# Layer A's product of probabilities and v of pairs 0 to 4, placed before the end of the next pair's key projection

## The chip, the cores and the metric

The kernel runs on one core of a Trainium2 chip. A core has TensorE (PE, with its weight loads as a row of their own, PEld), VectorE (DVE), ScalarE (ACT), GpSimd (POOL) and SyncE (SP), whose queue issues nearly all DMAs here. The metric is the device time of one execution in microseconds, as the median of several runs. A profile is one further execution, recorded by the hardware profiler.

## The reference

The reference is a block of two layers on a sequence of 512 tokens, 1024 wide, in float32. Each layer is RMS norm, an input projection, a mixer over 16 heads of 64, a gate, an output projection and a residual. Layer A, in which the change lies, is attention over dilated windows, for three groups of heads (`g`) that are merged by their softmax denominators:

```python
proj = hn @ w_in                                   # q, k, v of three groups, and the gate
q = rms_norm(q, q_gain[g]); k = rms_norm(k, k_gain[g])
logits = q @ k.T * scale + bias                    # keys within the window of group g
p = exp(logits - max); denom = sum(p)
out = (p @ v) / denom
...
y = sum(alpha[g] * out[g]) * silu(gate)            # alpha: softmax over the groups' log denominators
x = x + y @ w_out
```

Layer B is a neighbourhood attention on an 8 x 64 grid of the same tokens. The change does not touch it.

## The kernel before

**Numbers.** A matrix product of the projections is made of three TensorE matmuls: each operand is split into a high part in fp32r and the rest, and high x high, high x rest and rest x high are summed in PSUM (`mm3`, L232). Three such matmuls of 128 x 128 by 128 x 512 are one step below. The weights come by DMA in raw pieces (`wraw`, L191), ScalarE or VectorE casts them (`wh`, L127), and VectorE or POOL subtracts (`wl`, L133). There are four buffers for `wh` and four for `wl`.

**Layer A's main work.** The sixteen heads are done as eight pairs (`hc` 0 to 7). For a pair, `main_a` (L628) runs in this order: the key projection (`project_qk` with "rawk", 8 values of k times 4 token tiles, 32 steps, which also makes v of groups 1 and 2), the query projection ("rawq", 32 steps), the projection of v of group 0 (`v0_a`, L589, 8 steps) and that of the gate (`gate_a`, L578, 8 steps). In a projection of keys or queries the four token tiles accumulate in the four banks of the pool `ps_acc`; at the last k, after each step, ScalarE evacuates its tile (`evac`, L504, with the activations of L530), and POOL squares it for the norm of the heads. `v0_a` and `gate_a` take a bank of the same pool each (L299).

**Layer A's side work.** Beside this runs the attention of the pair before. The queries and keys of a pair go through DRAM to be turned (`move_q`, L684: a write at L691, four reads at L697); then `split_q` (L736) scales them on ScalarE. `attn_a` (L886) makes the scores in two halves `u` of two token tiles each, both heads side by side, in the four banks of the pool `ps_side` (`bank`, L78), with the softmax on VectorE (L929, L940, L801) and ScalarE (L951, L802). The probabilities are turned by VectorE (L865) and by a write and four reads through DRAM for each half (`turner.send`, L874 and L878). What remains of a pair is put off in the list `pending`: the product of the turned probabilities with v (`weigh`, L962, 52 matmuls into two banks of `ps_side`), then `whole` (L778: a ScalarE copy and a VectorE add that empty the two banks) and `put_y` (L804: the product with the gate on VectorE, y's high part by ScalarE at L827, the rest by POOL at L828).

**What sets the order.** TensorE's order is the order of the text. The others are ordered by the library's scheduler with a simulated timeline (`schedule_with_timeline_sim=True`), but for instructions that `keep_in_program_order` pins behind the one before them on their engine. Main and side work are two Python generators. Main yields after each step; `run` (L1032) then lets the side go on if its due time has come. Time is `clock`, which the helper `matmul` (L222) advances by a modelled duration: 640 for a step, 2,880 for the product of a pair, 1,600 for half of its scores. A side generator gives a number (wait so long), nothing (1,200) or

```python
yield "wait", ("rawk", hc + 1), 5200
```

that is: until 5,200 after the clock at which ("rawk", hc + 1) was stamped, at the end of the key projection of pair `hc + 1`. `later_on` puts DMAs and a few other jobs at a clock as well. `moved(hc)` is true for pairs 0 to 5.

In `attn_a(hc)` of pairs 1 to 5 the first thing done was the product of the pair before, so its place was the beginning of the query projection of pair `hc + 1`, ahead of the first half of the scores of pair `hc`. The product of pair 5 stands in another branch, that of pair 6 too.

Of the kernel before, what the change touches and what calls it, by code (L numbers as in the profile page):

```python
# [51 lines left out]
def tile_hybrid_encoder(  # L52
# [193 lines left out]
    def later_on(delay, job):  # L246

        timers.append((clock[0] + delay, job))
        timers.sort(key=lambda t: t[0])
# [172 lines left out]
    def square_a(k):  # L422
        nc.scalar.activation(x_all[:, k, :], x_all[:, k, :], AF.Square)
# [462 lines left out]
    def attn_a(hc):  # L886
# [7 lines left out]
        def scores(u):  # L894

            tiles = []
            for t in (2 * u, 2 * u + 1):
                cs, n = (64, 192) if t == 0 else (0, 192) if t == 3 else (0, 256)
                tiles.append((t, [bank("log") for _ in range(2)], cs, n))
            for t, lgs, cs, n in tiles:  # L900
                ks = slice(P * t + cs, P * t + cs + n)
                parts = [(0, j, slice(cs, cs + n), k0[:, ks]) for j in range(4)] + [
                    (1 + g, j, slice(256 + P * g, 384 + P * g), qt[:, :, 4 + g, 32 * j : 32 * j + 32])
                    for g in range(2)
                    for j in range(4)
                ]
                for g, j, cols, keys in parts:
                    for hd in range(2):
                        hs = slice(64 * hd, 64 * hd + 64)
                        matmul(  # L910
                            lgs[hd][32 * j : 32 * j + 32, cols],
                            qt[hs, t, g, 32 * j : 32 * j + 32],
                            keys[hs],
                            share=2,
                            start=(g == 0),
                            stop=(g == 2),
                        )
            return [
                (hd, t, softmax(hd, t, lgs[hd], cs, n)) for t, lgs, cs, n in tiles for hd in range(2)
            ]  # L920
# [34 lines left out]
        def turn_p(hd, t, pr):  # L955
            tp = bank("tp")
            for i in range(4):
                transpose(tp[:, i * P : (i + 1) * P], pr[:, i * P : (i + 1) * P])
            dst = sb(pts[0], at(t, 0, hd, 0), [[128, 2], [32, 2], [512, 4], [1, 32]])
            nc.vector.tensor_copy(dst, tp.rearrange("p (g i a r) -> p g i a r", g=2, i=2, a=4))  # L960
# [31 lines left out]
        if hc < NHC - 1:  # L992
            for u in range(2):
                if moved(hc):
                    if pending and u == 0:
                        pending.pop(0)()
                        yield
                    yield "wait", ("rawk", hc + 1), 5200 if u == 0 else 16800 if hc else 12500
                else:
                    yield 6500 if u == 0 else 7000  # L1000
                turned = turner(512)
                turners.append(turned)
                for hd, t, pr in scores(u):
                    turned.put(pr, 512, 256 * hd + 64 * (t % 2), 128)
                send = partial(turned.send, pq[:, 2048 * u : 2048 * u + 2048], *((6000, 500) if u else (8500, 1200)))
                later_on(7000 + 2000 * u, send)
                if pending and u == 0:
                    yield 5000
                    pending.pop(0)()
            pending.append(lambda: put_y(hc, weigh(), True, False))  # L1010
        else:
            for u in range(2):
                if u == 0:
                    yield "wait", ("gate", hc), 500
                yield 600
                held = scores(u)
                yield 3200
                if pending:
                    yield "wait", ("gate", hc - 1), 16800
                    pending.pop(0)()  # L1020
                    yield
                for args in held:
                    turn_p(*args)
                    yield
            yield from v_a(hc)
            stamp["ya", "turned"] = 0
            put_y(hc, weigh(), True, True)
            yield

    pending = []  # L1030
# [258 lines left out]
    def side():  # L1289
        for k in range(KT):  # L1290
            norm(0, k, x_all[:, k, :])
            if k:
                square_a(k - 1)
            stamp["na", k] = 0
            if k == 4:
                gains()
            yield 1000
        square_a(KT - 1)
        for k in range(1, KT):
            yield 1300  # L1300
            nc.vector.tensor_add(x_all[:, 0, :], x_all[:, 0, :], x_all[:, k, :])
        yield 1500
        row_scale(row_sums(x_all[:, 0, :]))
        y = big.tile([P, 2 * KT * S], F32R, tag="y", name="y").rearrange("p (n k t) -> p n k t", n=2, k=KT)
        st["y_h"], st["y_l"] = y[:, 0], y[:, 1]
        yield 2500
        bias_lines()
        later_on(21000, lambda: st.__setitem__(("e", 0), bias_a(0)))
        yield 2500
        scales_a()  # L1310
        first_out()
        stamp["rs", "a"] = 0
        for hc in range(NHC):
            if hc < NHC - 1:
                yield from k_a(hc)
                yield from chain(q_a(hc), v_a(hc))
                if moved(hc):
                    yield from st.pop(("land", hc))
                yield from attn_a(hc)
                if hc == 1:  # L1320
                    bias_rows()
            else:
                gap[0] = cycle((500, 500, 700))
                yield from chain(q_a(hc), k_a(hc))
                yield from attn_a(hc)
        yield from residual(xg, 0)
        yield from residual(xg, 4)
        stamp["ya", KT - 1, "y"] = 0
        yield "wait", ("x", KT - 1), 800
        for f in range(KT):  # L1330
            square_b(f)
            yield 600
        yield 4500
        row_scale(row_sums(st.pop("ssq")))
        stamp["rs", "b"] = 0
        yield 5000
        nc.scalar.mul(rs_half, spread(), 0.5)
        stamp["rs", "all"] = 0
        for job, hc, delay in B_PLAN:
            yield "wait", ("b", "start"), delay  # L1340
            if job == "scores":
                yield from side_b(hc)
                continue
            yield "wait", ("back", hc), 3500
            if hc == NHC - 2:
                stamp["yb", "turned"] = 0
            pending.pop(0)()
            yield
            if hc >= NHC - 2:
                yield from residual(xm_d, 4 * (hc % 2))  # L1350

    run(main(), side())


# [98 lines left out]
```

## Time and profile before

| | before |
|---|---|
| median of 3 runs | 815.26 us (815.03 to 816.6) |
| the profiled execution | 817.6 us |
| its span, from the first instruction to the last | 815.8 us |
| TensorE busy (matmuls) | 808.5 us, 99% |
| VectorE busy | 532.0 us, 65% |
| ScalarE busy | 434.6 us, 53% |
| POOL busy | 246.9 us, 30% |
| DMA | 169.33 MB, mean 208 GB/s |
| layer A's pairs 1 to 4, from one product to the next | about 62 us each |

A line of the profile names the source line, the engine, the operation, the tiles written and read (`acc<-wh,hn_h`), shapes and counts. `acc` are the projections, `log` the scores, `o` the product, `tp` transposes on TensorE, `p` the probabilities. The busy time of TensorE counts each matmul from its start to a modelled end, and matmuls overlap; a busy share of 99% therefore does not say that TensorE never waits. The chain of waits shows better where it does: it goes from the last instruction back to whatever each step waited for. In brackets stands how long an engine was idle before an instruction, and what ended that.

### The profile page before, as it was taken

Reading aid. Unit: us, or ns where it says so; the run is one execution under the profiler, and the core shown is the slowest. Engines: PE = TensorE matmul, PEld = TensorE weight load, DVE = VectorE, ACT = ScalarE, POOL = GpSimd, SP = SyncE. Lnnn points to the kernel's source line nnn. Section 1 sums busy time; section 2 is a strip of 40 time slices with the busy share of each in tenths; the row PEclk is TensorE's granted clock in tenths of the full one; section 3 lists DMA queues with packets and bytes.
Section 4 is the critical chain, followed back from the end, with each engine's and each line's share of the span. In section 5 each row is a group of like instructions: output and inputs, shape, how many; then the busy total and the mean of one; then the engine's idle time right before and its main releaser. Section 6 shows DMA issues by size and latency. Waiting matters only on the chain.

```text
span 815.8 us, 16172 instructions
## 1 busy us (share of the span) xinstructions
PE 808.5 (99%) x5972; PEld 662.2 (81%) x5972; DVE 532.0 (65%) x1364; ACT 434.6 (53%) x913; POOL 246.9 (30%) x400
## 2 busy tenths in 40 slices
PE   9999999999999999999999999999999999999998
PEld 7888888788888888888788888888888887778787
DVE  7466575665576576477476765538656989897824
ACT  7352752752752752662662564536337665757821
POOL 2262441542441441441432342111221315040100
PEclk9999999999999999999999999999999999999999
DMA  7367879779879779968858555157353887698664
GB/s 261 106 207 232 224 216 266 208 200 301 210 210 316 195 220 292 240 186 277 226 164 233 179 160 135 41 193 250 119 164 129 245 230 213 200 268 244 174 213 155
DMA packets 86478, 169.33 MB, mean 208 GB/s; under 512 B 7504, under 2 KB 45520, under 8 KB 86400
## 3 DMA queue, kind: packets, MB, share of 16 engines
q1 hardware_dynamic: 86256, 168.04, 70.0%
q8 instruction: 47, 0.77, 0.4%
q10 hardware_dynamic: 144, 0.26, 0.1%
q14 instruction: 31, 0.25, 0.1%
HBM read 126.21 MB, written 48.22 MB: 214 GB/s over the span
## 4 chain that ended last, share of the span: by engine, by line
PE 92%; DVE 3%; ACT 3%; DMA 1%; issue 1%; SPq 0%; DVEq 0%
PE acc L226 82%; PE log L226 5%; PE o L226 4%; ACT p L1222 1%; PE tp L230 1%; ACT p L1228 1%; DVE wl L133 1%; DMA eb<-eb_d 1%; DMA x_all<-in_xt 0%; DVE rawq L330 0%; DVE rawq L716 0%; PE pa L226 0%; DVE tr L865 0%; ACT wh L127 0%; PE pk L226 0%
## 5 line engine op out<-in xcount | busy, mean ns | idle before, releaser
L226 PE MATMUL acc<-wh,hn_h 128*128 128x512 f32 x704 | 278.8, 397 | 1.2 <-ACT hn_h L419 0.8
L226 PE MATMUL acc<-wl,hn_h 128*128 128x512 f32 x704 | 274.4, 391 | 0.0
L226 PE MATMUL acc<-wh,hn_l 128*128 128x512 f32 x704 | 274.3, 390 | 0.0
L127 ACT CAST wh<-wraw 128x512 fp32r<-128x512 f32 (+1 forms) x240 | 146.2, 613 | 227.0 <-PE acc L226 204.1
L133 DVE TENSOR_TENSOR wl<-wraw,wh 128x512 fp32r<-128x512 f32 (+1 forms) x169 | 121.7, 721 | 132.8 <-ACT wh L127 131.7
L133 POOL TENSOR_TENSOR wl<-wraw,wh 128x512 fp32r<-128x512 f32 (+1 forms) x72 | 94.3, 1310 | 237.8 <-ACT wh L127 228.4
L226 PEld LDWEIGHTS acc<-wh,hn_h 128*128 128x128 f32 x704 | 132.6, 189 | 32.9 <-issue 3.3
L226 PEld LDWEIGHTS acc<-wh,hn_l 128*128 128x128 f32 x704 | 132.7, 189 | 28.0
L226 PEld LDWEIGHTS acc<-wl,hn_h 128*128 128x128 f32 x704 | 132.8, 189 | 26.3
L308 POOL TENSOR_TENSOR sq<-rawq 128x256 f32<-128x256 f32 (+1 forms) x80 | 63.4, 806 | 87.1 <-ACT rawq L530 76.3
L226 PE MATMUL acc<-y,wh 128*128 128x512 f32 (+1 forms) x272 | 81.5, 383 | 0.0
L226 PE MATMUL acc<-hn_h,wh 128*128 128x512 f32 x192 | 75.5, 393 | 0.0
L226 PE MATMUL acc<-hn_l,wh 128*128 128x512 f32 x192 | 74.7, 389 | 0.0
L226 PE MATMUL acc<-hn_h,wl 128*128 128x512 f32 x192 | 74.7, 389 | 0.0
L865 DVE STREAM_TRANSPOSE tr<-p 128x512 f32<-128x512 f32 (+1 forms) x88 | 58.2, 677 | 19.8 <-ACT p L1228 9.0
L311 DVE TENSOR_REDUCE ss<-sq 128x4 f32<-128x256 f32 (+1 forms) x96 | 48.3, 505 | 34.3 <-POOL sq L308 27.4
L951 ACT ACTIVATE p<-p,mn 128x512 f32<-128x512 f32 (+1 forms) x64 | 44.9, 702 | 25.5 <-DVE mn L940 25.5
L226 PEld LDWEIGHTS acc<-y,wh 128*128 128x128 f32 x272 | 48.8, 188 | 9.4 <-issue 0.9
L330 DVE TENSOR_TENSOR rawq<-rawq,rs 128x256 f32<-128x256 f32 (+1 forms) x96 | 51.2, 593 | 5.3 <-POOL rs L119 4.9
L226 PE MATMUL acc<-y,wl 128*128 128x512 f32 (+1 forms) x136 | 51.3, 377 | 0.0
L530 ACT ACTIVATE rawq<-acc,rs_n 128x512 f32<-128x512 f32 (+1 forms) x76 | 44.2, 611 | 0.7 <-PE acc L226 0.2
L802 ACT ACTIVATE p<-p,mn 128x512 f32<-128x512 f32 (+1 forms) x64 | 43.4, 699 | 0.8 <-DVE mn L801 0.7
(142 smaller groups left out, 950.2 us busy)
## 6 DMA issues: line engine op xcount, KB each, us to landing
wraw<-in_w SPq DMA_DIRECT2D x111, 512.0 KB, 5.3
td<-tr SPq DMA_DIRECT2D x14, 1024.0 KB, 6.2
pt<-td SPq DMA_DIRECT2D x56, 256.0 KB, 6.4
qd<-rawq SPq DMA_DIRECT2D x6, 1536.0 KB, 6.6
qt<-qd SPq DMA_DIRECT2D x24, 384.0 KB, 7.4
td<-tr SPq DMA_DIRECT2D x8, 896.0 KB, 4.8
pt<-td SPq DMA_DIRECT2D x32, 224.0 KB, 6.5
v0x<-in_w SPq DMA_DIRECT2D x8, 512.0 KB, 6.0
```

The lines of the kernel that those rows point to most:

```text
L127: nc.scalar.copy(h, raw)
L133: eng.tensor_sub(l, raw, h.bitcast(F32))
L226: nc.tensor.matmul(o, l, r, **kw)
L230: nc.tensor.transpose(o, i, ident)
L308: nc.gpsimd.tensor_mul(sq.rearrange("p (f a r) -> p a f r", a=4, r=32), v, v)
L311: nc.vector.tensor_reduce(ss[:, i * ns : (i + 1) * ns], sq.rearrange("p (a b) -> p a b", b=64), axis=AX.X, op=ALU.add)
L330: m = nc.vector.tensor_mul(v, v, by)
L530: nc.scalar.activation(dst, src, AF.Copy, scale=rs_n[:, i : i + 1])
L802: nc.scalar.activation(pr, pr, AF.Copy, scale=mn[:, 3:4])
L865: nc.vector.transpose(dst, src[:, :n].rearrange(order, b=4, k=32, **({"g": 2} if apart else {})))
L951: nc.scalar.activation(row, row, AF.Exp, bias=mn[:, 1:2], scale=-1.0, accum_out=mn[:, 2:3])
L1222: nc.scalar.activation(pr[:, o : o + n], pr[:, o : o + n], AF.Exp, bias=mn[:, 0:1], scale=-1.0, accum_out=mn[:, 2:3])
```

## The change

Two edits. The product leaves its place at the start of `attn_a`; in its stead `side` gives it a wait of its own, 18,500 after the stamp of the gate of pair `hc`, between the turning of that pair's queries (`q_a`) and the point where they are split (`land`). `pending` is empty for pair 0; for pairs 1 to 5 it holds the product of the pair before.

```diff
@@ attn_a, for u in range(2)
                 if moved(hc):
-                    if pending and u == 0:
-                        pending.pop(0)()
-                        yield
                     yield "wait", ("rawk", hc + 1), 5200 if u == 0 else 16800 if hc else 12500
                 else:
                     yield 6500 if u == 0 else 7000
@@ side, for hc in range(NHC)
                 yield from k_a(hc)
                 yield from chain(q_a(hc), v_a(hc))
                 if moved(hc):
+                    if pending:
+                        yield "wait", ("gate", hc), 18500
+                        pending.pop(0)()
+                        yield
                     yield from st.pop(("land", hc))
                 yield from attn_a(hc)
```

The gate's stamp of pair `hc` falls at the end of its gate projection, and the key projection of pair `hc + 1` follows directly.

## Prediction

> **What bounds the kernel now.** I read the page first, then the chain of waits in stretches, then the timelines of ScalarE, TensorE and its weight loads, and last the DMA rows. The page:
>
> ```profile
> span 815.8 us, 16172 instructions
> PE 808.5 (99%) x5972; PEld 662.2 (81%) x5972; DVE 532.0 (65%) x1364; ACT 434.6 (53%) x913; POOL 246.9 (30%) x400
> ...
> PE 92%; DVE 3%; ACT 3%; DMA 1%; issue 1%; SPq 0%; DVEq 0%
> ...
> q8 instruction: 47, 0.77, 0.4%
> ```
>
> TensorE holds 92% of the chain. Only a microsecond in which TensorE stands still more, or less, can move the end; what the other engines do counts when TensorE waits for it. I write S(n) for the scores of pair n; the product of pair n-1 now stands just before them. These are pieces of the chain around S(0), S(1), S(2), S(3), S(4) and S(5), each line with start, length, what:
>
> ```profile
> 92.17 1.84 PE log L226 x96
> ...
> 149.85 1.59 PE acc L226 x6
> 151.44 1.53 PE log L226 x68
> 152.98 0.78 issue
> 153.76 0.66 PE log L226 x28
> 154.41 10.43 PE acc L226 x45
> ```
>
> ```profile
> 214.52 1.95 PE log L226 x88
> ...
> 226.88 1.96 PE log L226 x90
> 228.84 43.08 PE acc L226 x189
> 276.62 1.84 PE log L226 x96
> ```
>
> ```profile
> 338.58 2.29 PE log L226 x82
> ...
> 396.28 3.11 PE o L226 x104
> ...
> 400.98 1.57 PE log L226 x75
> 402.55 1.05 issue
> 403.61 0.63 PE log L226 x21
> ...
> 420.88 0.44 PE tp L230 x4
> ```
>
> Three things are to be seen. A plain stretch of projection runs at 43.08 / 189 = 0.228 us a multiplication, so one step (three multiplications, the unit in which the program yields) is 0.684 us. The product costs 3.11 us (396.28) and six multiplications later (149.85) the first half of the scores follows. That half, 1.84 us where nothing disturbs it (S(0), S(3)), takes 2.97 us at S(1), 1.95 at S(2), 2.29 at S(4) and 3.25 at S(5). So the place where the product now stands costs 1.13 + 0.11 + 0 + 0.45 + 1.41 = 3.1 us of standing TensorE in all, and no more than that can come back.
>
> Who ends these waits? At S(4) the profile names it (weight loads), at S(1) and S(5) it says "issue", which is waiting for nothing that it shows; but one block of code lands on the instruction queue in each of the windows 151.05 to 151.25 and 401.0 to 401.2, ahead of exactly these two breaks:
>
> ```profile
> 339.74 0.15 PEld L226 LDWEIGHTS log<-k,qt 64*32 64x32 f32 x11 [0.33 <-DVE ow L782]
> ```
>
> ```profile
> q8 instruction: 1, 0.02, 33.8%
> ```
>
> ```profile
> q8 instruction: 1, 0.02, 30.0%
> ```
>
> L782 empties the product's banks, which the second score tile takes over. The 47 blocks of 0.77 MB are 16 KB each; TensorE's 2 x 5972 records over 47 blocks make 254 to a block, and product, six multiplications and scores (104 + 6 + 96, with as many weight loads) burn 412 of them in 3.11 + 1.59 + 1.84 us, a block in 4.0. I read the two breaks as TensorE outrunning its code.
>
> **The change, part by part.** The product is 52 matmuls, and the same 52 are still issued; nothing is added or removed but the order. By the helper's clock a step counts 640, the product 2,880, half the scores 1,600.
>
> *Where it lands.* The wait is 18,500 after the gate of the same pair; a projection starts at that stamp, so it is over at step 29 (18,560), the first of the last k's four. Strictly the first evacuation is already issued, the other three follow. The product moves up by 3 steps of that projection and the 3 that stand between its end and the product: about 4.1 us.
>
> *Its gain.* Product and second score half no longer follow each other: 3 remaining steps plus 9 (below) lie between. The banks of L782 are free long before, so the 0.45 and 0.11 go. Any 254 records now hold at least 46 of projection beside the product's 208, so a block lasts 23 x 0.228 + 3.11 = 8.4 us and no longer 4.0; the 1.13 and 1.41 go too. Gain 3.1 us. It may be as little as 0.56, if the two breaks are no code.
>
> [...]
>
> *What the product leaves behind at its new place.* Four instructions follow it: a ScalarE copy and a VectorE add (L781, L782), a multiply, a ScalarE copy of y (L827), and a subtraction on POOL. ScalarE has three evacuations still to do.
>
> ```profile
> 275.07 0.59 ACT L781 COPY ow<-o 128x512 f32<-128x512 f32 x1 [1.29 <-PE o L226]
> 277.13 1.13 ACT L827 CAST y<-gt 128x512 fp32r<-128x512 f32 x1 [1.48 <-DVE gt L822]
> ```
>
> Evacuation 1 is ready 0.68 us after the product, when L781 is done; its bank is wanted by the next projection 3 + 1 steps after the product, 2.7 us. There is a microsecond to spare, so I take nothing. If y's copy were queued ahead of it, ScalarE would be done with that only 277.13 + 1.13 - 275.07 = 3.2 us after the product and the evacuation at about 3.9: 1.2 us a pair, 6 us over five. Of the two the evacuation is ready first, so I leave this to the upper end. POOL's subtraction goes ahead of the norm of the keys, which is not used before 11,000 on the helper's clock. The new wait holds up only the side program, and what stands behind it there (the split of the queries) waits for the later stamp of the key projection anyway.
>
> *What it does to the scores.* This is the part that decides. S(n)'s two halves wait for 5,200 and 16,800 after the stamp of the key projection, and the clock also counts the product. Before: 3 steps, product (2,880), 2 steps, scores at 6,080; then 15 steps (the 45 multiplications at 154.41), second half after 5 + 15 = 20 of the 32 steps of the query projection, 12 to go. After: the product lies ahead of the stamp, so the first half comes after 9 steps (5,760), the second after 9 + 15 = 24. Only 8 are to go. S(0), which has no product in front of it, shows this already: its first half at 92.17 comes 9 steps after the projection's end.
>
> Behind the second half ScalarE has a softmax to do, and then the query projection's evacuations. At S(2), whose second half ends at 228.84:
>
> ```profile
> 229.45 0.73 ACT L951 ACTIVATE p<-p,mn 128x512 f32<-128x512 f32 x1 [1.85 <-DVE mn L940]
> ...
> 233.55 0.71 ACT L802 ACTIVATE p<-p,mn 128x512 f32<-128x512 f32 x1
> 234.16 0.60 ACT L127 CAST wh<-wraw 128x512 fp32r<-128x512 f32 x1
> 234.67 0.72 ACT L802 ACTIVATE p<-p,mn 128x512 f32<-128x512 f32 x1
> 235.29 0.61 ACT L127 CAST wh<-wraw 128x512 fp32r<-128x512 f32 x1
> 235.80 2.40 ACT L530 ACTIVATE rawq<-acc,rs_n 128x512 f32<-128x512 f32 x4
> ```
>
> ```profile
> 237.08 0.39 PE L226 MATMUL acc<-hn_h,wh 128*128 128x512 f32 x1
> ```
>
> ```profile
> L530 ACT ACTIVATE rawq<-acc,rs_n x4: 672/682/695, 111.1 to 112.8; 128x512 f32<-128x512 f32 x4
> ```
>
> The first evacuation starts 6.96 us after the scores and is over at 235.80 + 0.68 = 236.48. TensorE wants that bank at 237.08 for the v projection: the four accumulator banks are all held by the query projection. So the margin is 0.60 us, and the change takes 4 x 0.684 = 2.74 us from it. ScalarE is busy without a hole from 229.45 on, so its time does not shrink; only one of the two casts falls away, because the buffer it fills is given back only when the projection ends. The evacuation then starts 6.96 - 0.51 = 6.45 us after the scores and ends at 7.13, and TensorE arrives at 8 x 0.684 = 5.47: it waits 1.66 us.
>
> Does ScalarE really let the older softmax go first, though the evacuation has been ready? Layer B shows the same meeting, with the wait:
>
> ```profile
> 713.42 0.80 ACT L1228 ACTIVATE p<-p,mns 128x256 f32<-128x256 f32 x2
> 714.13 0.60 ACT L127 CAST wh<-wraw 128x512 fp32r<-128x512 f32 x1
> 714.64 2.40 ACT L530 ACTIVATE rawq<-acc,rs_n 128x512 f32<-128x512 f32 x4
> ```
>
> ```profile
> 714.58 0.39 PE L226 MATMUL acc<-wh,hn_l 128*128 128x512 f32 x1
> 715.37 0.50 PE L226 MATMUL acc<-wh,hn_h 128*128 128x512 f32 x1 [0.40 <-ACT rawq L530]
> ```
>
> TensorE's next multiplication, due at 714.81, starts at 715.37, 0.05 us after the first evacuation ends (714.64 + 0.68). That evacuation had been ready since three steps before 714.81, and normalises (L1228) and a cast went ahead of it.
>
> The second halves of S(1) to S(5) are moved alike: five waits. At S(5) two groups of transposes of 0.44 us each follow the scores, one of them now before the end of the projection, which leaves 1.22. Cost 4 x 1.66 + 1.22 = 7.9 us. Lower bound: the evacuation slips in ahead of the last normalise, in the hole where the cast stands (start 5.83, end 6.51): 4 x 1.04 + 0.60 = 4.8. Upper: both casts stay ahead: 4 x 2.17 + 1.73 = 10.4.
>
> *DMAs.* No transfer is removed. The reads of the turned probabilities hang on the second half, 2.7 us later, and the product that needs them is 4.1 us earlier. SP issues the last two of pair 4 here; their product starts at 396.28:
>
> ```profile
> 379.04 1.56 SPq L878 DMA_DIRECT2D pt<-td  x2
> ```
>
> ```profile
> pt<-td SPq DMA_DIRECT2D x56, 256.0 KB, 6.4
> ```
>
> They are in by about 380.6 + 6.4 = 387.0, 9.3 us early; 2.5 us stay. They also fall behind the write of the queries (L691) on SP's queue. I take nothing, and a rival below.
>
> **The sum.** -3.1 + 7.9 = +4.8 us. On the profiled execution, 817.6 us with a span of 815.8, that makes 822.4; on the median of the runs, 815.26, it makes **820.0**. With the bounds of the evacuation: 815.26 - 3.1 + 4.8 = 817.0, and 815.26 - 3.1 + 10.4 = 822.6. About 0.2% (1.6 us) is what a measurement of this kernel can tell from no change.
>
> **Rivals.**
> *ScalarE takes the evacuations first* (faster). The order of ScalarE comes from the library's simulated timeline, not from the text; if its softmax has a hole early enough, the evacuation goes in and only the gain is left: 815.26 - 3.1 = 812.2. For it: the cast at 234.16 did slip in ahead of the last normalise. Against: that is 5.3 us after the scores, when TensorE stands at the bank already, and ScalarE has no hole before it. 0.19.
> *Gain and wait cancel.* A wait of about 0.6 us a pair, half of my lower bound, if the softmax runs shorter at its new place: 815.26 to within 1.6. 0.11.
> *The two breaks stay*, because TensorE waits there for something other than code: gain 0.56 only, 815.26 - 0.56 + 7.9 = 822.6. The rows of the instruction queue speak against it. 0.07. [...]
> *The product waits for its probabilities*: decides where the last read lands over 2.5 us later than now, behind the query write. Each microsecond beyond that, in five pairs, adds 5: 825.0. Median landings are in time; 0.06.
> *The wait for 18,500 lands elsewhere*, at a step more or less: neither gain nor cost changes by more than 0.7 us a pair, and the scores hang on the stamp in any case. No chance of its own.
>
> **How the numbers follow.** My forecast, with its own range from 817.0 to 822.6, has 0.57; with the two rivals behind it slower has 0.70, the same 0.11, faster 0.19. The range reaches down to the faster case, 812.0, since without it two in ten and the tails would be out, and up to 825.0.
>
> **What would show it.** Right: first score halves of S(1) to S(5) all near 1.84 us; 24 steps between the end of the key projection and the second half; then, at the start of each v projection of pairs 2 to 6, a TensorE wait of 1 to 2 us that ends with ACT rawq L530, about 7.1 us after the scores. Wrong: that wait missing because L530 stands among the L951 and L802 rows; a TensorE wait ahead of the product that a DMA ends; or "issue" breaks that have only moved.

## The result and the profile after

| | before | after |
|---|---|---|
| median | 815.64 us (815.03 to 817.21, 6 runs) | 828.4 us (823.88 to 830.66, 6 runs) |
| the profiled execution, its span | 817.6 us, 815.8 us | 830.3 us, 828.5 us |
| granted TensorE clock, mean of the profiled execution | 1.000 | 0.994 |

The ratio is 1.0149, with a 95% interval of 1.0119 to 1.0179: slower, as forecast, but by 12.8 us and not by 4.8, and outside the range. The page of the kernel after, the lines that answer to those of before, and the group of the first matmuls of the v and gate projections:

```profile
span 828.5 us, 16170 instructions
...
PE 813.5 (98%) x5972; PEld 665.1 (80%) x5972; DVE 539.9 (65%) x1364; ACT 434.8 (52%) x913; POOL 248.8 (30%) x400
...
PE 77%; ACT 7%; DVE 7%; DMA 6%; issue 2%; POOL 0%; SPq 0%; ACTq 0%; DVEq 0%
...
L226 PE MATMUL acc<-hn_h,wh 128*128 128x512 f32 x192 | 78.1, 407 | 9.7 <-ACT rawq L530 9.7
```

TensorE's share of the chain falls from 92% to 77%; ScalarE, VectorE and DMAs take over what it loses. The last column of the last line says where TensorE stands: 9.7 us, all of it ended by the evacuation of the queries (L530). TensorE's timeline shows them one by one, at the v projections of pairs 2 to 6, behind S(1) to S(5); in brackets the idle time and what ended it:

```profile
176.82 0.50 PE L226 MATMUL acc<-hn_h,wh 128*128 128x512 f32 x1 [3.07 <-ACT rawq L530]
...
241.39 0.50 PE L226 MATMUL acc<-hn_h,wh 128*128 128x512 f32 x1 [0.69 <-ACT rawq L530]
...
305.70 0.50 PE L226 MATMUL acc<-hn_h,wh 128*128 128x512 f32 x1 [2.02 <-ACT rawq L530]
...
371.60 0.58 PE L226 MATMUL acc<-hn_h,wh 128*128 128x512 f32 x1 [2.07 <-ACT rawq L530]
...
437.68 0.50 PE L226 MATMUL acc<-hn_h,wh 128*128 128x512 f32 x1 [1.80 <-ACT rawq L530]
```

The brackets sum to 9.65. They count from a modelled end, 0.39 us after the start of the matmul before; at the pitch of 0.228 each wait is 0.16 longer, so TensorE loses 9.65 + 5 x 0.16 = 10.45 us, where the forecast had 7.9.

That is not all of it. The view by stretches of 3.41 us, the length for which the granted clock stays down each time (the columns are stretch, its length, the busy time of PE, PEld, DVE, ACT and POOL, PEclk, DMA share, GB/s):

```profile
173.90:177.31 3.41, 0.49 (x2) 0.45 (x3) 2.19 (x5) 3.41 (x8) 0.56 (x2) 1.00 0.50 160
177.31:180.72 3.41, 3.41 (x10) 2.66 (x9) 1.97 (x3) 2.29 (x5) 3.35 (x4) 0.50 0.00 0
303.60:307.02 3.42, 1.40 (x7) 1.10 (x7) 2.48 (x6) 3.42 (x8) 1.38 (x3) 1.00 0.46 102
307.02:310.43 3.41, 3.41 (x10) 2.67 (x9) 1.38 (x4) 2.08 (x4) 3.41 (x4) 0.50 0.00 0
...
436.72:440.14 3.42, 2.46 (x13) 2.06 (x14) 3.42 (x6) 3.42 (x7) 2.37 (x3) 1.00 0.57 164
```

Behind three of the five waits TensorE runs at half clock for 3.41 us. There a matmul comes every 0.43 us instead of every 0.228, as TensorE's timeline shows:

```profile
178.29 0.63 PE L226 MATMUL acc<-hn_l,wh 128*128 128x512 f32 x1
178.72 0.63 PE L226 MATMUL acc<-hn_h,wl 128*128 128x512 f32 x1
```

So 8 matmuls go where 15 would, and 7 x 0.228 = 1.6 us are lost each time, 3 x 1.6 = 4.8 us in all. Behind the other two waits, 0.69 and 1.80 us (the last line of the stretches holds about half of the second), it keeps its clock, 1.00.

The gain is there. The first halves of S(1) and S(5), TensorE's timeline; from the start of the last projection matmul ahead to the first one behind:

```profile
153.53 0.39 PE L226 MATMUL acc<-wh,hn_l 128*128 128x512 f32 x1
153.85 0.56 PE L226 MATMUL log<-k,qt 64*32 64x192 f32 x16
...
155.69 0.50 PE L226 MATMUL acc<-wh,hn_h 128*128 128x512 f32 x1
...
415.21 0.39 PE L226 MATMUL acc<-wh,hn_l 128*128 128x512 f32 x1
...
417.37 0.50 PE L226 MATMUL acc<-wh,hn_h 128*128 128x512 f32 x1
```

Both take 2.16 us, and the half itself 1.84 (153.85 to 155.69), where before had 2.97 and 3.25. The sum against the profiled execution of before: -3.1 + 10.45 + 4.8 = +12.15; the spans differ by 828.5 - 815.8 = 12.7. The rest is a slow start: behind each wait the second matmul follows after some 0.33 us and not 0.228, 0.1 us five times. So the profile accounts for the time. Why the waits are longer than worked out, and why the clock falls behind some of them only, these rows don't say.

### The profile page after: what moved, and what is told of

Its sections match the earlier page's. It is cut to its first block, busy times and chain, and to the rows that moved or that the text cites. A ratio compares the mean times of both kernels' runs of the same rounds, so it can differ in the third digit from the quotient of the medians.

```text
span 828.5 us, 16170 instructions
## 1 busy us (share of the span) xinstructions
PE 813.5 (98%) x5972; PEld 665.1 (80%) x5972; DVE 539.9 (65%) x1364; ACT 434.8 (52%) x913; POOL 248.8 (30%) x400
## 4 chain that ended last, share of the span: by engine, by line
PE 77%; ACT 7%; DVE 7%; DMA 6%; issue 2%; POOL 0%; SPq 0%; ACTq 0%; DVEq 0%
PE acc L226 69%; PE o L226 4%; DMA e<-l_d 3%; PE log L226 3%; DVE wl L133 2%; ACT p L951 2%; DMA vv<-vd 1%; DVE rawq L330 1%; ACT rawq L530 1%; PE tp L230 1%; ACT wh L127 1%; ACT p L1219 1%; ACT p L802 1%; DMA rp<-in_rpb 1%; DVE p L929 1%
## 5 line engine op out<-in xcount | busy, mean ns | idle before, releaser
L133 DVE TENSOR_TENSOR wl<-wraw,wh 128x512 fp32r<-128x512 f32 (+1 forms) x169 | 131.3, 779 | 145.5 <-ACT wh L127 145.2
L133 POOL TENSOR_TENSOR wl<-wraw,wh 128x512 fp32r<-128x512 f32 (+1 forms) x72 | 95.1, 1320 | 251.5 <-ACT wh L127 242.1
L308 POOL TENSOR_TENSOR sq<-rawq 128x256 f32<-128x256 f32 (+1 forms) x80 | 65.6, 834 | 104.5 <-ACT rawq L530 94.7
L226 PE MATMUL acc<-hn_h,wh 128*128 128x512 f32 x192 | 78.1, 407 | 9.7 <-ACT rawq L530 9.7
L865 DVE STREAM_TRANSPOSE tr<-p 128x512 f32<-128x512 f32 (+1 forms) x88 | 58.4, 679 | 31.0 <-ACT p L802 19.0
L226 PE MATMUL acc<-hn_h,wl 128*128 128x512 f32 x192 | 76.8, 400 | 0.0
L226 PE MATMUL acc<-hn_l,wh 128*128 128x512 f32 x192 | 76.6, 399 | 0.0
L951 ACT ACTIVATE p<-p,mn 128x512 f32<-128x512 f32 (+1 forms) x64 | 44.9, 702 | 42.8 <-DVE mn L940 40.5
L226 PEld LDWEIGHTS acc<-hn_h,wh 128*128 128x128 f32 x192 | 37.3, 194 | 19.8 <-ACT rawq L530 11.8
L330 DVE TENSOR_TENSOR rawq<-rawq,rs 128x256 f32<-128x256 f32 (+1 forms) x96 | 49.9, 579 | 3.8 <-POOL rs L119 3.4
L530 ACT ACTIVATE rawq<-acc,rs_n 128x512 f32<-128x512 f32 (+1 forms) x76 | 44.2, 608 | 1.9 <-PE acc L226 1.6
```

The lines of the kernel that those rows point to most:

```text
L133: eng.tensor_sub(l, raw, h.bitcast(F32))
L226: nc.tensor.matmul(o, l, r, **kw)
L308: nc.gpsimd.tensor_mul(sq.rearrange("p (f a r) -> p a f r", a=4, r=32), v, v)
L330: m = nc.vector.tensor_mul(v, v, by)
L530: nc.scalar.activation(dst, src, AF.Copy, scale=rs_n[:, i : i + 1])
L865: nc.vector.transpose(dst, src[:, :n].rearrange(order, b=4, k=32, **({"g": 2} if apart else {})))
```

## The experiments

Steps are counted in the 32 steps of the query projection: before, the halves of the scores stand behind steps 5 and 20, after, behind 9 and 24. All edits are in the wait of `attn_a`, unless said otherwise. The kernel before ran beside each group of four: 815.41 us (20 runs) beside the first, 814.96 (23 runs) beside the second, 814.92 (31 runs) beside the third.

### First group: is it the place of the scores, the bank, the clock?

**Both halves back to their old steps, the product at its new place** (after, edited):

```diff
-5200 if u == 0 else 16800 if hc else 12500
+(3000 if hc else 5200) if u == 0 else 13920 if hc else 12500
```

> The product stays at its new place, and the two halves of the scores of pairs 1 to 5 go back to steps 5 and 20 of the query projection (waits of 3,000 and 13,920 instead of 5,200 and 16,800). Theory of the late scores: the loss comes from the second half's softmax standing 4 steps later in front of the query projection's evacuations, so it is gone, and the 3.1 us that the scores lost behind the product are gained: 811.5 to 813.5 us, granted clock 1.000, no wait of TensorE for L530 at the v projections. Rival, the product's own copies and sums disturb the evacuations at the new place: the loss stays, 824 to 830 us.

Measured: 819.08 us (817.44 to 819.31, 9 runs), ratio 1.0038 (1.0024 to 1.0053), clock 1.000. The waits for L530 are gone, and so is most of the loss, but the time is 6 us above what I expected. The weight loads and TensorE at S(2) show why, with the rows in order of time from two filters of the timeline:

```profile
213.62 0.39 PE L226 MATMUL acc<-wh,hn_l 128*128 128x512 f32 x1
214.31 0.66 PE L226 MATMUL log<-k,qt 64*32 64x192 f32 x16 [0.30 <-ACT k L758]
...
216.82 0.50 PE L226 MATMUL acc<-wh,hn_h 128*128 128x512 f32 x1
```

```profile
214.91 0.18 PEld L226 LDWEIGHTS log<-qt 64*32 64x32 f32 x16 [0.33 <-ACT qt L758]
```

From 213.62 to 216.82 are 3.20 us instead of 2.16, in all five pairs alike: 5 x 1.04 = 5.2 us. The scores wait for ScalarE to scale keys and queries (L758). In the kernel before, the 3.11 us of the product ran ahead of these scores. My edit had uncovered a wait that the product used to hide; -3.1 + 5.2 = +2.1 against a span 817.4 - 815.8 = 1.6 longer.

**Both halves late, the product at its old place** (before, edited; steps 9 and 24 as in after):

```diff
-5200 if u == 0 else 16800 if hc else 12500
+(8500 if hc else 5200) if u == 0 else 19500 if hc else 12500
```

> The kernel before, with the product where it was, and only the two halves of the scores of pairs 1 to 5 put off to steps 9 and 24 (waits of 8,500 and 19,500). Theory of the late scores: five waits for L530 at the v projections of about 2 us each (10 us in sum, as in the changed kernel), the granted clock falls after those over 2 us, and since six steps now lie between product and scores most of the 3.1 us is gained as well: 823 to 831 us. Rival, the product's new place does the harm: 812 to 817 us.

Measured: 828.16 us (825.68 to 834.8, 4 runs), ratio 1.0171 (1.0133 to 1.0208). The profiled execution waits for L530 at all five v projections, 0.89, 2.63, 2.46, 2.09 and 1.25 us, 9.3 in sum, though its clock stays at 1.000. The place of the scores is enough for the whole harm; within the spread of these four runs the product's new place by itself costs nothing that can be seen.

**Another bank for v** (after; the v projections of pairs 2 to 6 accumulate in `ps_side`):

```diff
-        acc.append(ps_acc.tile([P, 512], F32, tag="acc", name="acc"))
+        acc.append(bank("acc") if side else ps_acc.tile([P, 512], F32, tag="acc", name="acc"))
...
-        yield from project_t(acc)
+        yield from project_t(acc, 2 <= hc <= 6)
```

> The changed kernel, but the v projections of pairs 2 to 6 accumulate in a bank of the scores' pool, which is free by then, and not in a bank of the query projection. The evacuations may be as late as they like. Theory of the late scores with the bank as its link: the five waits and the falls of the clock go, 811.5 to 814 us, clock 1.000. Rival, TensorE waits there for something else that ends at the same time (weights, VectorE): 824 to 830 us.

Measured: 816.6 us (814.08 to 818.87, 12 runs), ratio 1.0013 (0.9998 to 1.0028). The bank is the link between the late softmax and TensorE; without it the time is 1.2 us above before instead of 12.8. About 3 us less than expected come back, since the late softmax then shows one place further on, at the product of pair 1, which waits for its probabilities:

```profile
203.09 0.43 PE L226 MATMUL o<-pt,rawk 64*64 64x128 f32 x4 [0.77 <-issue]
204.41 2.51 PE L226 MATMUL o<-pt,rawk 64*64 64x128 f32 x58 [0.88 <-DMA pt<-td]
```

A stretch of half clock follows (granted clock 0.68 from 204 to 208), the only one in this profile; with it this one place costs some 3.5 us. This is the rival "the product waits for its probabilities", hidden in the kernel after by the longer wait ahead of it.

**Matmuls to fill the wait** (after; six unused 128x512 matmuls ahead of the v projections of pairs 2 to 6, 6 x 0.228 = 1.4 us, so that TensorE stands still for less of each wait):

```diff
+        if 2 <= hc <= 6:
+            fill = bank("fill")
+            for _ in range(6):
+                nc.tensor.matmul(fill, wide(P), wide(S), start=True, stop=True)
         yield from project_t(acc)
```

> The changed kernel with six matmuls of 128 x 512 into an unused bank ahead of each v projection of pairs 2 to 6 (6 x 0.228 = 1.4 us), which run while TensorE would wait for L530. Theory of the clock: the halved clock (3.41 us each time, 1.7 us lost) follows a wait of 2 us or more; with the filler no wait is longer than 3.07 - 1.4 = 1.7 us, so the clock stays at 1.000, and 5.1 us come back against 0.5 us of filler that pair 2's short wait does not hide: 822 to 825 us with waits that are as late as before. Rival, the clock falls for another reason (the load, the time of day): 0.994 to 0.997 and 826 to 831 us.

Measured: 823.09 us (822.02 to 827.52, 6 runs), ratio 1.0104 (1.0081 to 1.0127): 7.7 us above the kernel before beside it, where after stood 12.8 above, by giving TensorE more to do. The profiled execution, 827.5 us, is the slowest, with a clock of 0.998, and has one stretch of half clock, behind the wait of S(1); the other five have a clock of 1.000 and 822.0 to 824.2. So giving TensorE useless work in the waits, with the evacuations as late as before, took 5 us off: the clock's share is real.

### Second group: which half, and what makes it late?

**The first half alone late** (before, edited; steps 9 and 20):

```diff
-5200 if u == 0 else 16800 if hc else 12500
+(8500 if hc else 5200) if u == 0 else 16800 if hc else 12500
```

> The kernel before with one edit: the first half of the scores is released 8.5 us of the plan after the keys instead of 5.2, so that it stands where it stands in the kernel after; the product of probabilities with v stays in the query projection, the second half stays at its old place. Theory A (the gain of about 3.1 us comes from where the first half stands, not from where the product stands): 811.5 to 814 us. Theory B (the gain needs the product out of the query projection): 815 to 816.5 us, no change.

Measured: 824.65 us (823.21 to 825.54, 4 runs), ratio 1.0119 (1.009 to 1.0148). Neither theory: 10 us slower, with the second half where it always stood, and waits for L530 of 1.07, 2.73, 2.51, 2.57 and 0.55 us. The longest:

```profile
237.91 0.50 PE L226 MATMUL acc<-hn_h,wh 128*128 128x512 f32 x1 [2.73 <-ACT rawq L530]
```

**The second half back, the first left at step 9** (after, edited; steps 9 and 20):

```diff
-5200 if u == 0 else 16800 if hc else 12500
+5200 if u == 0 else 14100 if hc else 12500
```

> The kernel after with one edit: the second half of the scores of pairs 1 to 5 is released 14.1 us of the plan after the keys instead of 16.8, which is its old step, 20 of 32; the first half stays where the kernel after has it. Theory A (the loss is the second half's lateness alone, and the gain of 3.1 us is independent of it; what was left in the run with both halves back was the first half, too early for the scaled keys and queries of L758, 0.9 us a pair): 811.5 to 814 us, clock 1.000, no wait of TensorE for L530 ahead of the v projections, no wait for L758. Theory B (something else of the new order costs some 4 us in every version that has the product in the key projection): 816 to 819 us.

Measured: 824.31 us (822.84 to 827.89, 5 runs), ratio 1.0114 (1.0086 to 1.0141); waits of 1.8 us at S(1) to S(4), 0.17 at S(5):

```profile
306.82 0.50 PE L226 MATMUL acc<-hn_h,wh 128*128 128x512 f32 x1 [1.78 <-ACT rawq L530]
```

Neither theory again. With these two the reason that my forecast gave falls: moving the second half back by 2.7 us a pair should have ended every wait of 1.66, and takes their sum from 9.65 to 7.36 only; and with the first half late they come in the kernel before too.

**ScalarE's copy of v later** (after, edited in `move_v`). `place` (L619) copies v of group 0 at a time of its own on the helper's clock:

```diff
-out, back, there = (26000, 32000, 38000) if moved(hc) else (8000, 13000, 18500)
+out, back, there = (26000, 32000, 42000) if moved(hc) else (8000, 13000, 18500)
```

> The kernel after with one edit: ScalarE's copy of v (L619) is set 4 us of the plan later, so that it no longer stands in the softmax of the first half. Theory A (that copy makes VectorE late for the second half's softmax in pairs 2 to 5, and this makes the waits for L530 2.0 to 2.2 us instead of some 1.5, long enough for the clock to fall): the waits of S(3) to S(5) fall by about 0.5 us each and two of three stretches at half clock go, 823 to 825.5 us. Theory B (the copy is beside the point; VectorE is late for its own work): 826.5 to 830 us, waits as before.

Measured: 817.78 us (817.36 to 819.69, 11 runs), ratio 1.0038 (1.0024 to 1.0051), clock 1.000. More than theory A expected: 2.8 us above before are left of 12.8, by moving a copy of 0.6 us. First ScalarE in the kernel after, in the softmax of the first half of S(3) and S(4):

```profile
290.87 0.60 ACT L127 CAST wh<-wraw 128x512 fp32r<-128x512 f32 x1
291.38 0.61 ACT L619 COPY v0x<-vv 128x512 f32<-128x512 f32 x1
291.90 1.33 ACT L802 ACTIVATE p<-p,mn 128x512 f32<-128x512 f32 x2
...
357.78 0.62 ACT L619 COPY v0x<-vv 128x512 f32<-128x512 f32 x1 [0.83 <-DMA vv<-vd]
```

The copy stands between the exponentials and the last two normalises, and at S(4) it waits for a DMA there. In after it starts 7.2 to 8.9 us after the first scores of S(1) to S(5), ahead of these normalises; in the kernel before it starts 8.8 us after them or later, behind. VectorE behind it, after:

```profile
292.65 1.33 DVE L865 STREAM_TRANSPOSE tr<-p 128x512 f32<-128x512 f32 x2 [1.49 <-ACT p L802]
293.91 1.39 DVE L330 TENSOR_TENSOR rawq<-rawq,rs 128x256 f32<-128x256 f32 x4
295.21 0.68 DVE L133 TENSOR_TENSOR wl<-wraw,wh 128x512 fp32r<-128x512 f32 x1
295.82 1.30 DVE L566 STREAM_TRANSPOSE rawq<-rawq 128x512 f32<-128x512 f32 x2
297.04 1.59 DVE L133 TENSOR_TENSOR wl<-wraw,wh 128x512 fp32r<-128x512 f32 x1
298.56 0.41 DVE L929 CUSTOM_DVE_ANT_0 p<-log,e 128x256 f32<-128x256 f32 x1
```

and with the copy moved:

```profile
286.50 1.33 DVE L865 STREAM_TRANSPOSE tr<-p 128x512 f32<-128x512 f32 x2 [0.97 <-ACT p L802]
...
290.88 0.65 DVE L133 TENSOR_TENSOR wl<-wraw,wh 128x512 fp32r<-128x512 f32 x1
291.74 0.42 DVE L929 CUSTOM_DVE_ANT_0 p<-log,e 128x256 f32<-128x256 f32 x1 [0.21 <-PE log L226]
```

In after the row L929, with which the softmax of the second half begins, has no bracket: the scores were there, and VectorE came to them from its own queue, without a hole since 292.65. With the copy moved VectorE waits 0.21 us for the scores. It is the transposes (L865) that need the normalises, and the norm of the keys (L330), their turning (L566) and two weight pieces (L133) stand in the queue behind them.

The copy sets the transposes back by 0.5 to 0.7 us at S(1) to S(3), and by 1.4 and 1.5 at S(4) and S(5), where it waits for its DMA. The rest at S(3) comes from the last weight piece: it starts 13.31 us after the first scores instead of 12.60, falls behind one of GpSimd that starts at 13.08 in both kernels, and takes 1.59 us instead of 0.65 (GpSimd's row is in the last section). At S(4) and S(5) it takes 1.09 and 1.76 us in the same way; at S(1) and S(2) it starts ahead of GpSimd's, at 12.88 and 12.92, takes 0.65, and VectorE is at L929 in time. No run moved GpSimd's piece by itself.

**The copy and GpSimd's bias rows later** (after; the copy as above, and the work of `bias_rows` 9 us of the plan behind its load):

```diff
+        later_on(9000, partial(bias_rest, rp))
+
+    def bias_rest(rp):
+
         nc.gpsimd.tensor_scalar(rp, rp, -1.0, None, op0=ALU.mult)
```

The buffer `rp` got a tag of its own for it. It was tried because in the kernel after, at S(1), a load in flight held up GpSimd, its memsets for the softmax stood behind it, and ScalarE's exponential waited for these:

```profile
171.96 0.83 POOL L454 TENSOR_SCALAR rp<-rp 128x248 f32<-128x248 f32 x1 [3.43 <-DMA rp<-in_rpb]
172.74 0.24 POOL L928 MEMSET p<- 128x64 f32 x2
```

```profile
172.93 0.73 ACT L951 ACTIVATE p<-p,mn 128x512 f32<-128x512 f32 x1 [2.27 <-POOL p L928]
```

> The kernel after with two edits: ScalarE's copy of v (L619) 4 us of the plan later, and GpSimd's work on the bias rows (L454 and behind it) 9 us of the plan after its load, so that no memset of the softmax queues behind a load on its way. Theory A (these two are what the forecast's wait of 1.66 us lacked): the wait of S(1) falls from 3.2 to 1.5 to 2 us, those of S(3) to S(5) to 1.5 to 1.8, no stretch at half clock is left, 819 to 822 us, which is the forecast. Theory B (only the bias rows count): 823 to 826 us. Theory C (neither): 826.5 to 830 us.

Measured: 818.36 us (817.26 to 820.02, 12 runs), ratio 1.0042 (1.0027 to 1.0058): near the forecast, but no different from the copy moved alone. There L454 starts 16.1 us after the first scores of S(1), where after has 18.1, and the wait of S(1) is 1.02 us, 0.34 more than that of S(2). The copy is behind the wait of S(1) too: it stands in that softmax as well (the first row below, after). The turned probabilities are written 0.51 us later for it, and the bias load, two issues behind on SP's queue, is issued 0.51 us later (12.20 us after the first scores in after, the second row, and 11.69 with the copy moved, the third):

```profile
161.08 0.62 ACT L619 COPY v0x<-vv 128x512 f32<-128x512 f32 x1
```

```profile
166.05 0.80 SPq L453 DMA_DIRECT2D rp<-in_rpb  x1
```

```profile
163.71 0.79 SPq L453 DMA_DIRECT2D rp<-in_rpb  x1
168.16 0.84 POOL L454 TENSOR_SCALAR rp<-rp 128x248 f32<-128x248 f32 x1 [1.79 <-DMA rp<-in_rpb]
```

The load lands 18.0 to 18.6 us after the first scores in the three profiles with the product moved, the scores at 9 and 24 and the copy in place (after, the other bank, the filler), and 16.0 to 16.2 in the three with the copy moved. Why it is also longer on its way, 5.8 to 6.4 us instead of 4.3 to 4.5, stays open; what the bias rows cost by themselves was not told apart.

### Third group: the chain, and a better version

**The copy later and the second half back** (after; copy at 42000, waits 5200 and 14100, steps 9 and 20):

> The kernel after with two edits: ScalarE's copy of v (L619) 4 us of the plan later, and the second half of the scores back behind step 20, the first half left behind step 9. Theory A (VectorE reaches the second half's softmax some 13 us after the first half's scores, whatever the place of the second half's scores): waits for L530 of 0.4 to 1.2 us as with the copy moved alone, 816.5 to 819 us. Theory B (the place of the second half's scores sets it, and the copy was the whole rest): no waits, 811.5 to 814.5 us.

Measured: 820.29 us (818.63 to 820.76, 8 runs), ratio 1.005 (1.0032 to 1.0069). Theory A in kind, by its waits 0.1 us a pair and by the median 1.3 us over its numbers. The second half came 2.7 us earlier than with the copy moved alone, and the time did not improve. At S(3), whose first scores begin at 280.57 and whose last are over at 292.1, VectorE gets to the second half 12.9 us after the first scores, and TensorE waits:

```profile
293.50 0.41 DVE L929 CUSTOM_DVE_ANT_0 p<-log,e 128x256 f32<-128x256 f32 x1
```

```profile
301.79 0.51 PE L226 MATMUL acc<-hn_h,wh 128*128 128x512 f32 x1 [1.32 <-ACT rawq L530]
```

The starts of S(3) in these kernels, read from the timelines, in us after the first half's scores begin:

| kernel | steps of the halves | VectorE at the second half (L929) | first evacuation (L530) | wait at v |
|---|---|---|---|---|
| before | 5, 20 | 13.7 | 21.3 | none |
| after | 9, 24 | 14.8 | 21.2 | 2.02 |
| both halves back, product moved | 5, 20 | 14.4 | 21.9 | none |
| both halves late, product not moved | 9, 24 | 15.2 | 21.6 | 2.46 |
| first half alone late | 9, 20 | 14.2 | 21.7 | 2.51 |
| second half back | 9, 20 | 13.5 | 21.0 | 1.78 |
| copy later | 9, 24 | 13.5 | 19.9 | 0.68 |
| copy later, second half back | 9, 20 | 12.9 | 20.5 | 1.32 |
| copy later, steps between | 7, 21 | 12.8 | 20.3 | none |

The evacuation comes 20 to 22 us after the first half's scores, wherever the second half's stand. TensorE wants the bank 19.8 us after them if they stand behind step 9, 21.1 behind step 7 and 22.5 behind step 5 (23.1 where the scores also wait for L758). So it is the first half that decides, through a chain over VectorE and ScalarE; where the second half stands behind step 24 the evacuation slips in ahead of the last normalise (6.4 us after L929), elsewhere it comes behind it (7.5 us).

**The steps between, with the copy later** (after; copy at 42000, and):

```diff
-5200 if u == 0 else 16800 if hc else 12500
+(4200 if hc else 5200) if u == 0 else 15000 if hc else 12500
```

> The kernel after with two edits: ScalarE's copy of v (L619) 4 us of the plan later, and the halves of the scores released at 4.2 and 15.0 us of the plan instead of 5.2 and 16.8, which puts them behind steps 7 and 21 of the query projection (after: 9 and 24, before: 5 and 20). Theory A (the first half's softmax, VectorE's work between the halves and the second half's softmax are one chain of some 13 us that must end ahead of the v projection; two steps earlier it ends in time, and the keys and queries are scaled by then): no wait for L530 above 0.3 us, none for L758, clock 1.000, profiled span 811.5 to 814, median 811 to 814 us. Theory B (the gain of 3.1 us, read from one profiled execution of before, is not there in the median run): no waits either, median 814 to 816 us, no change.

Measured: 813.38 us (812.54 to 815.17, 12 runs), ratio 0.9976 (0.9962 to 0.9991): faster than the kernel before, and than after. Its page:

```profile
span 812.6 us, 16166 instructions
...
PE 94%; DVE 3%; ACT 2%; DMA 0%; issue 0%; POOL 0%; DVEq 0%
...
L226 PE MATMUL acc<-hn_h,wh 128*128 128x512 f32 x192 | 76.2, 397 | 0.0
```

No wait for L530, none for L758. The span is 3.2 us shorter than that of the profiled execution of before, as theory A has it. By the ratio of the runs it is 0.24%, or 2.0 us, between 0.7 and 3.1: theory B, no gain at all, is excluded, if narrowly.

**The copy later and the other bank for v** (after, both edits as above):

> The kernel after with two edits: ScalarE's copy of v (L619) 4 us of the plan later, and the v projections of pairs 2 to 6 in a bank of the side group, which no evacuation holds. Theory A (the 4.2 us that were left with the copy moved are the wait for the bank; the other waits of the kernel with the side bank, 2 us ahead of the product for its probabilities, come from the same late softmax): no wait for L530 at the v projections, the product's wait under 1 us, clock 1.000, 812.5 to 815 us. Theory B (the late softmax shows in the product's wait all the same): 816 to 818 us.

Measured: 814.68 us (812.8 to 816.53, 12 runs), ratio 0.998 (0.9965 to 0.9995): theory A. What was left with the copy moved was the wait for the bank, and with the softmax in time the product waits for its probabilities at one place only, that of pair 3, some 0.65 us.

**The copy alone, in the kernel before** (before; copy at 42000):

> The kernel before with one edit: ScalarE's copy of v (L619) 4 us of the plan later. A control. Theory A (the copy did harm only where the first half's softmax met it, which in the kernel before it does not): 814 to 816.5 us, no change. Theory B (it delays that softmax in the kernel before too): under 813 us.

Measured: 815.42 us (813.48 to 817.25, 12 runs), ratio 0.9992 (0.9977 to 1.0007): no change. The copy does harm only where the first half's softmax meets it.

## Why the prediction was right in its direction and wrong in its size

**Right: the place of the product, and its price of nothing.** The product stands ahead of the last k's steps of the key projection, ScalarE takes two of the three evacuations that are left ahead of y's copy and the third behind it, TensorE waits there at none of the five places, and both halves late without it (828.16 us) cost as much as the whole change.

**Right in the profile, not settled in the runs: the gain of 3.1 us.** The breaks of S(1) and S(5) are gone in after. But 3.1 was read from one execution of before, 817.6 us where the median was 815.26, and with the copy moved in before, a profile shows one break of 0.5 us in the scores where before has two of 1.8 us together:

```profile
399.43 0.63 PE L226 MATMUL log<-qt 64*32 64x128 f32 x21 [0.55 <-issue]
```

How often they come was not measured; the version with steps 7 and 21 gains 2.0 us on the runs, between 0.7 and 3.1. My reading of them as code that arrives late agrees with the traces of before and after, but is not shown by them. The DMA records of the instruction queue give each block a start and a length, in before 151.11 and 1.08 us, 401.10 and 0.96. The two breaks end at 153.76 and 403.61, 1.57 and 1.55 us after their block's transfer has ended. In after the last blocks ahead of S(1) and S(5) start at 147.90 and 411.44 and take 1.03 and 1.11 us; they are in 4.9 and 3.0 us ahead of the scores (153.85 and 415.53), and there is no break. No run moved a block by itself.

**Right: that L530 makes TensorE wait, at five v projections.** Each wait stands there, and the other bank takes it away.

**Wrong: "The first evacuation then starts 6.96 - 0.51 = 6.45 us after the scores", the step from which 1.66 us a pair came.** It slid the ScalarE rows of S(2) rigidly along with the second half. Measured, it starts 8.0, 5.6, 7.0, 7.0 and 7.2 us after the scores of S(1) to S(5), and the waits cost 10.45 us instead of 7.9. At S(2) to S(5) the evacuation slips in ahead of the last normalise, the order of my lower bound, 4.8 us; that the sum still meets my upper one, 10.4, is luck. At S(2) itself the picture nearly holds: 0.69 + 0.16 = 0.85 us. Elsewhere the softmax did not begin with the scores. The first half had moved too, by four steps, and I looked only for what stands behind the second. Behind the first stand normalises, transposes, the norm of the keys and weight pieces, and into these fell a copy (L619) that keeps its own time on the helper's clock and so did not move along. At S(3) to S(5) this made VectorE 1.4 to 1.6 us late (14.8 to 15.0 instead of 13.5), half a microsecond and more by the copy and the rest by the weight piece that it pushed behind GpSimd's, and the wait some 2 us. At S(1) it made a load late that held up GpSimd and its memsets, and the wait 3.07. The copy's experiment and its control show it: with that copy out of the way the waits are 0.68 to 1.02 us in S(1) to S(4), and the time is 817.8, 2.2 us under my forecast; in the kernel before the copy's place is worth nothing. That the first half sets the end is shown by the three kernels with the halves behind 9 and 20: the second half stands where it stood before, and the waits are there.

**Missing: the clock.** The sum has no term for it; 4.8 us in the profiled execution, more than the 2.55 us by which the waits were too short. My waits were each to be 1.2 to 1.7 us, and waits of 1.3 us did not touch it (the version with the copy later and the second half back has a clock of 1.000). In after the waits of 2.02, 2.07 and 3.07 us cost another 1.6 each. A rival with its price in the clock would have been due: the profile of before has no stretch of half clock within layer A, so it could not show the price, and the range ended at 825.0.

**The rivals.** ScalarE did not take the evacuations first. The product's wait for its probabilities is real but hidden, and shows when the bank is freed. The two breaks did not stay, and gain and wait did not cancel.

## What to carry to other kernels

When a step moves, move everything that hangs on it in the forecast, and read the queues behind the first thing that moves, not only behind the last; ask too which jobs keep a time of their own and will now stand in the middle. A wait that a moved piece of work used to hide (here L758 under the product) comes up when the rest is put back. And a TensorE wait of some 2 us should be priced with the clock that it may lose: here three of 2.02 to 3.07 us cost 1.6 us more each, while one of 2.73 in another version cost none.

## What the runs showed of the hardware

**The granted clock fell for 3.41 us at a time, at points of one grid.** In the kernel after the falls begin at 177.31, 307.02 and 371.87 us: 38 and 19 times 3.413 us apart. My reading is that it matters how a wait lies in this grid; two waits fit it. In the profile of the kernel with the first half alone late, a wait of 2.73 us did not touch the clock. Its two stretches of the grid, found from the moment at which the clock first rises in that profile:

```profile
233.36:236.77 3.41, 1.81 (x9) 1.16 (x7) 2.09 (x5) 3.41 (x9) 0.85 (x3) 1.00 0.01 2
236.77:240.18 3.41, 2.27 (x10) 1.89 (x11) 2.06 (x4) 3.31 (x6) 2.96 (x4) 1.00 0.49 117
```

TensorE is idle for 1.60 us of the one and 1.14 of the other. In the kernel with the second half back a shorter wait, 1.8 us, lay within one stretch and cost the clock:

```profile
238.31:241.72 3.41, 1.63 (x7) 1.05 (x6) 2.67 (x4) 3.41 (x7) 1.96 (x3) 1.00 0.00 1
241.72:245.13 3.41, 3.41 (x9) 2.64 (x8) 2.06 (x3) 1.61 (x3) 3.41 (x4) 0.50 0.88 219
```

From 60 to 800 us of the kernel after, three stretches of the grid have 2.02, 2.07 and 2.92 us idle, and one at half clock follows each; no other has more than 0.96, and none of them has such a follower. In before the largest is 0.77, and the clock stays at 1.00. Of the stretches viewed in the other profiles, one with 2.01 us idle (the filler) and the one with 1.78 above were followed by half clock; one with 1.76 (both halves late) and those with 1.60 and 1.14 above were not. One case lies lower: with the other bank for v the clock fell behind two waits of 0.77 and 0.88 us, 1.65 in sum. The ends of matmuls are modelled, and each wait is some 0.16 us longer than its bracket (above), so these rows give no sharp limit. The clock first stands at its full value 10.39 us into the span of before and 10.06 into that of after; the difference, 0.33, is no multiple of 3.413, so the grid lies differently in the two spans. Whether it also lies differently from one execution of a kernel to the next was not measured; it would fit the six runs of after, whose clocks are 0.993 to 0.997. Those 0.004 of 828 us are 3.3 us, half of the 6.8 us over which the runs spread.

**A weight piece took 1.59 us on VectorE beside GpSimd.** The row at 297.04 above met this one of GpSimd; its like at 295.21, alone, took 0.68:

```profile
296.81 1.27 POOL L133 TENSOR_TENSOR wl<-wraw,wh 128x512 fp32r<-128x512 f32 x1 [3.96 <-ACT wh L127]
```

GpSimd's ends at 298.08, 1.04 us after VectorE's began, and VectorE's ends 0.55 us behind it. So it is at S(4) and S(5), where VectorE's ends 0.55 and 0.54 us behind GpSimd's. At S(1) and S(2) VectorE's is first and takes 0.65, and GpSimd's takes 1.60 and 1.65 instead of some 1.3. In all five the piece that starts second takes longer than such a piece alone; what holds it up no row shows.
